# A convolution with max pooling: warm-up products of a constant, two weight turns behind the first products, loads gated one by one

## The chip, the cores and the metric

The kernel runs on one core of a Trainium2 chip. The metric is the device time of one execution in microseconds. Lower is better.

## The reference

A 3x3 convolution with padding 1 over 16 images of 64 channels and 64x64 pixels gives 128 channels; then the maximum over 2x2 blocks is taken, all in float32.

```python
batch, c_in, h, w, c_out, k = 16, 64, 64, 64, 128, 3
...
conv[b, co] += weight[co, ci, kh, kw] * x_pad[b, ci, kh:kh+h, kw:kw+w]
...
output[b, c, i, j] = np.max(conv[b, c, i*pool_size:(i+1)*pool_size,
                                      j*pool_size:(j+1)*pool_size])
```

## The kernel before

**Tiling.** Two images lie together on the 128 partitions, 64 channels each, so a matmul takes 64 partitions and there is one for each half. The eight pairs of images are split into 4 "k" pairs and 4 "w" pairs, and every pair into 4 parts of 8 output rows; that gives 16 parts of each kind, numbered 0 to 15. An accumulator (`acc_0` to `acc_3`) holds one part of one parity of conv rows, for two images, in 4 KiB of each partition[...]. The list `free` hands them out and takes them back in program order.

**Arithmetic.** Even and odd conv rows are not computed each by itself. Combinations of rows (`ks`, `ws`, `we`, `wz`, `wy`, made from x on VectorE and GpSimd) meet combinations of the weights' three kernel rows: `G0` and `G2` are plain, `D2` is g2 - g1, `D0` is g0 - g1, and `GM` and `GP` are half of g0 + g2 minus or plus g1. One product step runs six matmuls for each block of weights (three column shifts, two image halves).

**Weights.** A block is put together in `wq`, turned on TensorE in four 128x128 transposes into an accumulator (`turn`, step "T" and the block's name) and copied to `wt` (`turn_out`, step "V" and the name).

**Steps.** The order of the whole program is written out by hand in the strings HEAD, STEADY and TAIL, and each engine runs its own instructions in that order. The steps that matter here are:

- `g0`, `g1`, `g2`: ScalarE casts of weight rows to `wq`. `D2`, `D0`, `GM`, `GP`: VectorE sums and differences (lines 350, 351, 354, 357). `GS`: GpSimd, g0 + g2 (line 352).
- `XO`, `XE`: VectorE casts of the odd and even rows of `kfirst`, the first 17 rows of the first k pair, to bfloat16 in `kx` (line 337). `X1`, `X2`: ScalarE casts of `ksecond`, the next 16 rows (line 344).
- `PA`, `PB`, `PR`: products of a k part: PA into one accumulator (12 matmuls), PB (12) and PR (6) into a second. `P2`, `P0` (6 each) go into the first accumulator of a w part, `P3`, `P1` (6 each) into its second. All are on line 183.
- `EV`/`ev`: ScalarE copies an accumulator to SBUF (line 286). `MX`/`mx`: VectorE takes the maximum of the second accumulator with it (line 299). `OD`/`od`: ScalarE copies the odd columns (line 304). `CM`/`cm`: VectorE takes the maximum over the columns, gives the accumulator back and sends the output (line 318). `SE`: ScalarE seeds a w part's second accumulator with minus the first (line 295).
- `KS`, `WS`, `E` on VectorE (E on GpSimd from part 5 on), `Z`, `Y` on GpSimd: the row combinations `ks`, `ws`, `we`, `wz`, `wy` (line 248). `on_gpsimd` makes Z and Y wait for the last `on_vector` instruction ahead of them in program order.

**Loads.** SP issues `wraw` (the weights), `kfirst`, then `wload(i)` for the parts of w pairs, and `ksecond`; they share one hardware queue. `kload` is issued by GpSimd and casts to bfloat16 as it loads. `behind(a, b)` makes instruction a wait for b. In the kernel before, `wload(0)` waits for the fourth of eight warm-up products and `ksecond` follows it; `wload(1)` to `wload(3)` wait for XO; the rest of the first k pair (`kload(0, ...)`) waits for E.0.

**Warm-up.** Eight products of a zeroed tile (line 135) run ahead of the first turn, two into each accumulator.

Of the kernel before, what the change touches and what calls it, by code (L numbers as in the profile page):

```python
# [11 lines left out]
def kernel(  # L12
# [21 lines left out]
    nc = tc.nc  # L34
    FP32 = mybir.dt.float32
    BF16 = mybir.dt.bfloat16
    MAX = mybir.AluOpType.max
    ADD = mybir.AluOpType.add
    SUB = mybir.AluOpType.subtract

    B, CI, H, W = x.shape
# [4 lines left out]
    NQ = 4  # L46
# [13 lines left out]

    acc = [psum.tile([128, 2, R, W], FP32, name=f"acc_{i}") for i in range(4)]
    free = deque(range(4))
    unset = set()

# [3 lines left out]
    def behind(inst, other):  # L70
        if other is not None:
            tc.add_manual_dep(inst.ins, other.ins.name, SYNC, reason="order")

    def on_vector(inst):
        sbuf_op[0] = inst
        return inst

    def on_gpsimd(inst):
        behind(inst, sbuf_op[0])
        return inst  # L80


    def rows_of(p, lo, hi):
        return x[2 * p : 2 * p + 2].rearrange("b c h w -> (b c) h w")[:, lo:hi, :]

    def chunk(q):
        return (2 * R * q + (q > 0), min(H, 2 * R * (q + 1) + 1))
# [4 lines left out]
    def kload(j, lo, hi):  # L92
        if j not in kx:
            kx[j] = kx_pool.tile([128, H, W], BF16, name="kx")
        return nc.gpsimd.dma_start(out=kx[j][:, lo:hi, :], in_=rows_of(2 * j, lo, hi))  # L95

    def wload(i):
        j, q = divmod(i, NQ)
        lo, hi = chunk(q)
        return nc.sync.dma_start(  # L100
            out=wx[j % 2][:, lo + 1 : hi + 1, :], in_=rows_of(2 * j + 1, lo, hi)
        )
# [6 lines left out]
    klo2, khi2 = chunk(1)  # L109
    ksecond = const.tile([128, khi2 - klo2, W], FP32)  # L110
# [10 lines left out]
    D2, G0, D0, G2, GM, G1, GP = range(1, 29, 4)  # L121
    BLOCKS = {"D2": D2, "G0": G0, "D0": D0, "G2": G2, "GM": GM, "G1": G1, "GP": GP}
    wq = const.tile([CO, 29, CI], BF16)
    wt = const.tile([128, 28, CO], BF16)
    gsum = const.tile([CO, 3, CI], FP32)
# [3 lines left out]
    g0, g1, g2 = wv[:, 0:3, :], wv[:, 3:6, :], wv[:, 6:9, :]  # L129

    def slots(m):
        return wq[:, m : m + 3, :]

    def zero(t, h):
        return nc.tensor.matmul(  # L135
            acc[t][:, h], zeros[:, 0:128], zeros, start=True, stop=True, skip_group_check=True
        )

    turned = {}

    def turn(m):
        t = free.popleft()
        turned[m] = t
        unset.add(t)
        tp = acc[t][:, 0].rearrange("p a b -> p (a b)").bitcast(BF16)
        lo, hi = BLOCKS[m] - 1, BLOCKS[m] + 3
        for j in range(lo, hi):
            nc.tensor.transpose(
                tp[:, (j - lo) * 128 : (j - lo + 1) * 128],
                wq[:, j : j + 2, :].rearrange("a b c -> a (b c)"),  # L150
                ident,
            )

    def turn_out(m):
        t = turned[m]
        free.append(t)
        lo, hi = BLOCKS[m] - 1, BLOCKS[m] + 3
        src = acc[t][:, 0].rearrange("p a b -> p (a b)").bitcast(BF16)[:, 0 : (hi - lo) * 128]
        dst = wt[:, lo:hi, :].rearrange("p a b -> p (a b)")
        if m == "GM":  # L160
            nc.scalar.mul(dst, src, 0.5)
        elif m == "GP":
            nc.vector.tensor_scalar_mul(out=dst, in0=src, scalar1=0.5)  # L163
        elif m in ("G0", "G1", "G2"):
            nc.scalar.copy(out=dst, in_=src)
        else:
            nc.vector.tensor_copy(out=dst, in_=src)  # L167
# [66 lines left out]
    def row_out(name, i):  # L234
        j, q = divmod(i, NQ)
        if (name, j) not in row:
            row[name, j] = row_pool.tile([128, HO, W], BF16, name=name)
        return row[name, j][:, q * R : (q + 1) * R, :]

    def row_in(t, first, pad):  # L240
        a = first + pad
        return t[:, a : a + 2 * R - 1 : 2, :]

    def row_op(engine, name, i, a, b, op):
        j, q = divmod(i, NQ)
        t, pad = (kx[j], 0) if name == "ks" else (wx[j % 2], 1)
        f = 2 * R * q
        return engine.tensor_tensor(  # L248
            out=row_out(name, i), in0=row_in(t, f + a, pad), in1=row_in(t, f + b, pad), op=op
        )  # L250

    def ks(i):
        on_vector(row_op(nc.vector, "ks", i, 0, 1, ADD))

    def ws(i):
        on_vector(row_op(nc.vector, "ws", i, 0, 1, ADD))
# [1 line left out]
    def we(i):  # L258
        if i < 5:
            inst = on_vector(row_op(nc.vector, "we", i, 1, 0, SUB))  # L260
            if i == 0:
                behind(kload(0, chunk(2)[0], H), inst)
        else:
            on_gpsimd(row_op(nc.gpsimd, "we", i, 1, 0, SUB))

# [69 lines left out]
    def cast_rows(first):  # L335
        inst = on_vector(
            nc.vector.tensor_copy(out=kx[0][:, first:khi:2, :], in_=kfirst[:, first:khi:2, :])  # L337
        )
        if first == 1:
            for i in range(1, NQ):  # L340
                behind(wload(i), inst)

    def cast_more(first):
        nc.scalar.copy(out=kx[0][:, klo2 + first : khi2 : 2, :], in_=ksecond[:, first::2, :])
# [2 lines left out]
        "g0": lambda: nc.scalar.copy(out=slots(G0), in_=g0),  # L347
        "g1": lambda: nc.scalar.copy(out=slots(G1), in_=g1),
        "g2": lambda: nc.scalar.copy(out=slots(G2), in_=g2),
        "D2": lambda: on_vector(nc.vector.tensor_sub(out=slots(D2), in0=g2, in1=g1)),  # L350
        "D0": lambda: on_vector(nc.vector.tensor_sub(out=slots(D0), in0=g0, in1=g1)),
        "GS": lambda: on_gpsimd(nc.gpsimd.tensor_tensor(out=gsum, in0=g0, in1=g2, op=ADD)),
        "GM": lambda: on_vector(
            nc.vector.tensor_sub(out=slots(GM), in0=gsum, in1=g1)  # L354
        ),
        "GP": lambda: on_vector(
            nc.vector.tensor_add(out=slots(GP), in0=gsum, in1=g1)  # L357
        ),
        "XO": lambda: cast_rows(1),
        "XE": lambda: cast_rows(0),  # L360
        "X1": lambda: cast_more(0),
        "X2": lambda: cast_more(1),
        "PA": pa, "PB": pb, "PR": pr, "P0": p0, "P1": p1, "P2": p2, "P3": p3,
        "KS": ks, "WS": ws, "E": we, "Z": wz, "Y": wy, "SE": seed,
        "EV": lambda i, h=None: evac(("k", i), h), "ev": lambda i, h=None: evac(("w", i), h),
        "MX": lambda i, h=None: rowmax(("k", i), h), "mx": lambda i, h=None: rowmax(("w", i), h),
# [3 lines left out]
    for m in BLOCKS:  # L370
        steps["T" + m] = lambda m=m: turn(m)
        steps["V" + m] = lambda m=m: turn_out(m)

    HEAD = """
        D2 g0 D0 g2 GS g1 TD2 VD2 TG0 VG0 XO TD0 VD0 TG2 VG2 TG1 VG1 XE GM PA.0 GP TGM VGM TGP
        KS.0 E.0 WS.0 PB.0 EV.0 X1 Z.0 Y.0 VGP P2.0 MX.0 SE.0 X2 PA.1 EV.1 WS.1 KS.1 E.1 PR.0
        P0.0 P3.0 Z.1 Y.1 OD.0 CM.0 P2.1 ev.0 PB.1 SE.1 mx.0 P0.1 P1.0 MX.1 P3.1 ev.1 od.0 PR.1
        WS.2 KS.2 E.2 Z.2 Y.2 OD.1 cm.0 CM.1 PA.2 EV.2 P2.2 PB.2 SE.2 mx.1 P1.1 P0.2 MX.2 P3.2
        od.1 ev.2 cm.1 E.3 KS.3 WS.3 Z.3 Y.3 PR.2 PA.3 OD.2 CM.2 P2.3 mx.2 EV.3 PB.3 SE.3 P1.2
# [12 lines left out]
    """  # L392
    FIRST, LAST = 4, 12

    for n in range(8):
        warm = zero(n // 2, n % 2)
        if n == 3:
            behind(wload(0), warm)
            nc.sync.dma_start(out=ksecond, in_=rows_of(0, klo2, khi2))
    kx[0] = kx_pool.tile([128, H, W], BF16, name="kx")  # L400

    def run(order):
# [44 lines left out]
```

## Time and profile before

| | |
|---|---|
| median of 6 runs | 107.76 us (107.58 to 108.36) |
| the profiled execution | 107.51 us |
| its span, from first to last instruction | 105.7 us |
| TensorE busy (matmuls) | 98.6 us, 93% of the span |
| VectorE, ScalarE, GpSimd busy | 82.7, 72.6, 60.2 us |
| granted TensorE clock, mean | 0.987 |
| moved by DMA | 21.96 MB, 208 GB/s in the mean |

The span is a little shorter than the time of the execution, since 1.81 us lie around it. In lines of the profile, L183 is a line of the kernel's source, and "out<-in" names what an instruction writes and reads; many steps share a line, since a helper issues them, so steps are told apart by their tiles and their order in time. A bracket behind a line is idle time ahead of an instruction and what ended it. Busy time of a matmul is modelled; the distance between starts is the better measure of its cost.

### The profile page before, as it was taken

How to read it: one execution, taken by the hardware profiler on the slowest of the kernel's cores; microseconds unless marked ns; L12 is line 12 of the kernel's file. 1: busy time of each engine (PE TensorE's matmuls, PEld its weight loads, DVE VectorE, ACT ScalarE, POOL GpSimd, SP SyncE). 2: the span in 40 equal slices, each digit the busy share in tenths (PEclk: the TensorE clock that was granted, in tenths of full speed). 3: DMA queues.
4: the chain of work that ended last, by engine and by line, in shares of the span. 5: the costliest groups of instructions: out<-in, count | busy, mean ns of one | idle time of the engine just before them, and what ended most of it. 6: DMA issues, size and time to landing. Idle time of an engine off the chain costs nothing.

```text
span 105.7 us, 2338 instructions
## 1 busy us (share of the span) xinstructions
PE 98.6 (93%) x900; PEld 45.3 (43%) x900; DVE 82.7 (78%) x113; ACT 72.6 (69%) x92; POOL 60.2 (57%) x69
## 2 busy tenths in 40 slices
PE   5989989999999999999999999999999999999810
PEld 2544344444454444444444444444444444455400
DVE  1599989889797868697887868687969878676950
ACT  4658966776767677767767676777776676775820
POOL 6206582914429494949476594949294856745000
PEclk9999999999999999999999999999999999999995
DMA  3999989899978679999955698999968412232052
GB/s 62 339 363 329 285 214 191 164 303 291 287 269 192 210 169 157 207 362 225 304 211 163 209 194 182 243 280 208 372 233 175 152 57 102 99 105 99 0 198 99
DMA packets 12475, 21.96 MB, mean 208 GB/s; under 512 B 944, under 2 KB 9136, under 8 KB 12464
## 3 DMA queue, kind: packets, MB, share of 16 engines
q1 hardware_dynamic: 11312, 18.03, 54.2%
q0 software_dynamic: 1008, 3.65, 19.6%
q8 instruction: 7, 0.11, 0.4%
q10 hardware_dynamic: 144, 0.13, 0.4%
q14 instruction: 4, 0.03, 0.1%
HBM read 17.07 MB, written 8.39 MB: 241 GB/s over the span
## 4 chain that ended last, share of the span: by engine, by line
PE 77%; DVE 13%; DMA 4%; issue 1%; ACT 1%; SPq 0%; DVEq 0%
PE acc L183 77%; DVE acc L299 6%; DMA kfirst<-in_x_dram 4%; DVE ws L248 2%; DVE kx L337 1%; DVE we L248 1%; DVE o L318 1%; DVE ks L248 1%; ACT od L304 1%; DVE wq L357 0%; DVE wq L354 0%; SPq L105 0%; DVE wt L163 0%; DVE wt L167 0%; DVEq L299 0%
## 5 line engine op out<-in xcount | busy, mean ns | idle before, releaser
L183 PEld LDWEIGHTS <-wt 64*128 64x128 bf16 x864 | 42.6, 94 | 51.5 <-issue 1.1
L299 DVE TENSOR_TENSOR acc<-acc,ev 128x1024 f32<-128x1024 f32 (+1 forms) x34 | 39.5, 1165 | 12.2 <-PE acc L183 11.9
L183 PE MATMUL acc<-kx,wt 64*128 64x504 bf16 (+3 forms) x384 | 46.2, 373 | 0.4 <-DVE kx L337 0.4
L286 ACT COPY ev<-acc 128x1024 f32<-128x1024 f32 (+1 forms) x34 | 32.6, 964 | 12.5 <-PE acc L183 11.0
L248 POOL TENSOR_TENSOR wz<-wx 128x512 bf16<-128x512 f32 x16 | 20.4, 1272 | 30.1 <-DVE ws L248 23.3
L304 ACT COPY od<-acc 128x512 f32<-128x512 f32 x32 | 18.8, 587 | 11.6 <-PE acc L183 11.5
L318 DVE TENSOR_TENSOR o<-acc,od 128x512 f32<-128x512 f32 x32 | 21.9, 690 | 3.6 <-ACT od L304 3.6
L248 POOL TENSOR_TENSOR wy<-wx 128x512 bf16<-128x512 f32 x16 | 20.3, 1270 | 0.0
L295 ACT ACTIVATE acc<-acc 128x1024 f32<-128x1024 f32 x16 | 16.1, 1008 | 1.3 <-PE acc L183 0.9
L248 POOL TENSOR_TENSOR we<-wx 128x512 bf16<-128x512 f32 x11 | 14.1, 1278 | 0.1
L183 PE MATMUL acc<-ws,wt 64*128 64x504 bf16 (+1 forms) x96 | 13.0, 377 | 0.4 <-DVE acc L299 0.4
L183 PE MATMUL acc<-we,wt 64*128 64x504 bf16 (+1 forms) x96 | 13.0, 377 | 0.3 <-DVE we L248 0.3
L183 PE MATMUL acc<-ks,wt 64*128 64x504 bf16 (+1 forms) x96 | 13.0, 377 | 0.1
L183 PE MATMUL acc<-wy,wt 64*128 64x504 bf16 (+1 forms) x96 | 13.0, 377 | 0.0
L183 PE MATMUL acc<-wz,wt 64*128 64x504 bf16 (+1 forms) x96 | 13.0, 377 | 0.0
L248 DVE TENSOR_TENSOR ws<-wx 128x512 bf16<-128x512 f32 x16 | 12.2, 764 | 0.0
L248 DVE TENSOR_TENSOR ks<-kx 128x512 bf16<-128x512 bf16 x16 | 6.7, 416 | 0.0
L95 POOL DMA_DIRECT2D kx<-in_x_dram x7 | 4.2, 594 | 3.2 <-DVE we L248 3.2
L135 PE MATMUL acc<-zeros 128*128 128x512 bf16 x8 | 3.3, 588 | 1.2 <-DVE zeros L112 1.2
L248 DVE TENSOR_TENSOR we<-wx 128x512 bf16<-128x512 f32 x5 | 3.4, 683 | 0.0
L350 DVE TENSOR_TENSOR wq<-wraw 128x192 bf16<-128x192 f32 x1 | 0.5, 501 | 2.5 <-DMA wraw<-in_weight_dram 2.5
L135 PEld LDWEIGHTS <-zeros 128*128 128x128 bf16 x8 | 1.0, 141 | 2.8 <-issue 1.7
(26 smaller groups left out, 16.8 us busy)
## 6 DMA issues: line engine op xcount, KB each, us to landing
out_dram<-o SPq DMA_DIRECT2D x31, 256.0 KB, 3.6
wx<-in_x_dram SPq DMA_DIRECT2D x8, 512.0 KB, 6.0
wx<-in_x_dram SPq DMA_DIRECT2D x4, 544.0 KB, 5.7
kx<-in_x_dram POOLq DMA_DIRECT2D x4, 496.0 KB, 8.1
wx<-in_x_dram SPq DMA_DIRECT2D x4, 480.0 KB, 5.2
kx<-in_x_dram POOLq DMA_DIRECT2D x3, 528.0 KB, 7.6
kfirst<-in_x_dram SPq DMA_DIRECT2D x1, 544.0 KB, 4.3
ksecond<-in_x_dram SPq DMA_DIRECT2D x1, 512.0 KB, 5.6
```

Of the source, the lines that this page charges most:

```text
L95: return nc.gpsimd.dma_start(out=kx[j][:, lo:hi, :], in_=rows_of(2 * j, lo, hi))
L135: return nc.tensor.matmul(acc[t][:, h], zeros[:, 0:128], zeros, start=True, stop=True, skip_group_check=True)
L183: nc.tensor.matmul(dst[:, half, i0:i1, o0:o1], wt[lo : lo + CI, m0 + kw - half, :], rows(lo, i0, i1, c0, c1), start=start and kw == 1, sto ...
L248: return engine.tensor_tensor(out=row_out(name, i), in0=row_in(t, f + a, pad), in1=row_in(t, f + b, pad), op=op)
L286: nc.scalar.copy(out=ev[g][:, halves(h)], in_=acc[ta[g]][:, halves(h)])
L295: nc.scalar.mul(acc[t], acc[ta["w", i]], -1.0)
L299: nc.vector.tensor_tensor(out=t, in0=t, in1=ev[g][:, halves(h)], op=MAX)
L304: nc.scalar.copy(out=od[g][:, halves(h)], in_=acc[tb[g]][:, halves(h), :, 1::2])
L318: nc.vector.tensor_tensor(out=o, in0=acc[tb[g]][:, s, :, 0::2], in1=od[g][:, s], op=MAX)
L337: nc.vector.tensor_copy(out=kx[0][:, first:khi:2, :], in_=kfirst[:, first:khi:2, :])
L350: "D2": lambda: on_vector(nc.vector.tensor_sub(out=slots(D2), in0=g2, in1=g1)),
```

## The change

- The eight warm-up products read a one-element constant, broadcast, that the program's start has written, and no longer the zeroed tile. `wload(0)` still waits for the fourth.
- The turns of G1 and GP move behind PB.0, into the two halves of one accumulator; VG1 moves from ScalarE to VectorE, and stands with VGP ahead of MX.0. An accumulator is given back by VGP and no longer by VG1 and VGP each.
- `ksecond` waits for D2; `wload(1)` waits for GM; `kload(0, ...)` waits for KS.0; `wload(2)` and `wload(3)` wait for E.0.
- In HEAD, GM comes ahead of XE, E.0 and WS.0 come behind TGP, SE.0 comes ahead of MX.0, and E.1 KS.1 WS.1 take the place of WS.1 KS.1 E.1.

```diff
+    def turned_cols(m):
+        lo, hi = BLOCKS[m] - 1, BLOCKS[m] + 3
+        tp = acc[turned[m]][:, int(m == "GP")].rearrange("p a b -> p (a b)").bitcast(BF16)
+        return lo, hi, tp[:, 0 : (hi - lo) * 128]
+
     def turn(m):
-        t = free.popleft()
-        turned[m] = t
-        unset.add(t)
...
+        turned[m] = turned["G1"] if m == "GP" else free.popleft()
+        unset.add(turned[m])
+        lo, hi, tp = turned_cols(m)
...
     def turn_out(m):
-        t = turned[m]
-        free.append(t)
...
+        if m != "G1":
+            free.append(turned[m])
+        lo, hi, src = turned_cols(m)
...
-        elif m in ("G0", "G1", "G2"):
+        elif m in ("G0", "G2"):
             nc.scalar.copy(out=dst, in_=src)
         else:
             nc.vector.tensor_copy(out=dst, in_=src)
...
     def ks(i):
-        on_vector(row_op(nc.vector, "ks", i, 0, 1, ADD))
+        inst = on_vector(row_op(nc.vector, "ks", i, 0, 1, ADD))
+        if i == 0:
+            behind(kload(0, chunk(2)[0], H), inst)
...
             if i == 0:
-                behind(kload(0, chunk(2)[0], H), inst)
+                for n in range(2, NQ):
+                    behind(wload(n), inst)
...
-        if first == 1:
-            for i in range(1, NQ):
-                behind(wload(i), inst)
+
+    def load_second(inst):
+        behind(nc.sync.dma_start(out=ksecond, in_=rows_of(0, klo2, khi2)), inst)
...
-        "D2": lambda: on_vector(nc.vector.tensor_sub(out=slots(D2), in0=g2, in1=g1)),
+        "D2": lambda: load_second(
+            on_vector(nc.vector.tensor_sub(out=slots(D2), in0=g2, in1=g1))
+        ),
...
-        "GM": lambda: on_vector(
-            nc.vector.tensor_sub(out=slots(GM), in0=gsum, in1=g1)
+        "GM": lambda: behind(
+            wload(1), on_vector(nc.vector.tensor_sub(out=slots(GM), in0=gsum, in1=g1))
         ),
...
     HEAD = """
-        D2 g0 D0 g2 GS g1 TD2 VD2 TG0 VG0 XO TD0 VD0 TG2 VG2 TG1 VG1 XE GM PA.0 GP TGM VGM TGP
-        KS.0 E.0 WS.0 PB.0 EV.0 X1 Z.0 Y.0 VGP P2.0 MX.0 SE.0 X2 PA.1 EV.1 WS.1 KS.1 E.1 PR.0
+        D2 g0 D0 g2 GS g1 TD2 VD2 TG0 VG0 XO TD0 VD0 TG2 VG2 GM XE PA.0 TGM GP KS.0 PB.0 VGM
+        EV.0 TG1 TGP E.0 WS.0 X1 P2.0 VG1 Z.0 Y.0 VGP SE.0 MX.0 X2 PA.1 EV.1 E.1 KS.1 WS.1 PR.0
...
+    ones = nc.const_aps.tensor(1.0, [128, 512], BF16)
     for n in range(8):
-        warm = zero(n // 2, n % 2)
+        warm = nc.tensor.matmul(
+            acc[n // 2][:, n % 2], ones[:, 0:128], ones, start=True, stop=True, skip_group_check=True
+        )
         if n == 3:
             behind(wload(0), warm)
-            nc.sync.dma_start(out=ksecond, in_=rows_of(0, klo2, khi2))
```

The set `unset`, which starts with all four accumulators after the change, decides only whether a seed step has to clear its accumulator with products of zeros first; no seed step does so before.

More of the change, by code (lines that the diff above doesn't have):

```diff
@@ L62 @@
     free = deque(range(4))
-    unset = set()
+    unset = set(range(4))
     SYNC = mybir.DependencyInfo(mybir.DependencyClass.Sync, mybir.DependencyReason.DATA)
@@ L139 @@
     turned = {}
+    def turned_cols(m):
+        lo, hi = BLOCKS[m] - 1, BLOCKS[m] + 3
+        tp = acc[turned[m]][:, int(m == "GP")].rearrange("p a b -> p (a b)").bitcast(BF16)
+        return lo, hi, tp[:, 0 : (hi - lo) * 128]
     def turn(m):
-        t = free.popleft()
-        turned[m] = t
-        unset.add(t)
-        tp = acc[t][:, 0].rearrange("p a b -> p (a b)").bitcast(BF16)
-        lo, hi = BLOCKS[m] - 1, BLOCKS[m] + 3
+        turned[m] = turned["G1"] if m == "GP" else free.popleft()
+        unset.add(turned[m])
+        lo, hi, tp = turned_cols(m)
         for j in range(lo, hi):
@@ L154, in turn_out @@
     def turn_out(m):
-        t = turned[m]
-        free.append(t)
-        lo, hi = BLOCKS[m] - 1, BLOCKS[m] + 3
-        src = acc[t][:, 0].rearrange("p a b -> p (a b)").bitcast(BF16)[:, 0 : (hi - lo) * 128]
+        if m != "G1":
+            free.append(turned[m])
+        lo, hi, src = turned_cols(m)
         dst = wt[:, lo:hi, :].rearrange("p a b -> p (a b)")
```

## The prediction

> **What bounds the kernel now.** I read the chain of waits first, then the timelines of single engines over the first 16 us. The chain (start, duration, what):
>
> ```profile
> 1.19 4.28 DMA kfirst<-in_x_dram
> 5.47 0.02 issue
> 5.49 0.43 DVE kx L337
> ...
> 9.44 1.23 DVE acc L299
> 10.67 1.87 DVE ws L248
> 12.54 0.34 DVE ks L248
> 12.88 0.61 DVE we L248
> 13.49 0.05 issue
> 13.53 77.55 PE acc L183 x720
> ```
>
> From 13.53 us on TensorE is the chain: 720 products in 77.55 us, 0.1077 us each, without a hole. What the change can win lies before 13.53, and it passes to the end one to one as long as that stretch stays dense. Two things hold the head: the landing of kfirst (5.47), and VectorE's row of work up to E.1 (the "we" that ends at 13.49). TensorE's timeline shows what they cost:
>
> ```profile
> 4.33 1.29 PE L148 MATMUL acc<-ident,wq 128*128 128x128 bf16 x20
> 5.97 1.39 PE L183 MATMUL acc<-kx,wt 64*128 64x512 bf16 x12 [0.36 <-DVE kx L337]
> 7.30 0.62 PE L148 MATMUL acc<-ident,wq 128*128 128x128 bf16 x8
> 7.85 1.47 PE L183 MATMUL acc<-kx,wt 64*128 64x512 bf16 x12
> ...
> 13.53 0.82 PE L183 MATMUL acc<-we,wt 64*128 64x512 bf16 x6 [0.32 <-DVE we L248]
> ```
>
> PA.0 starts at 5.97 (I call this t0). Up to P2.1 at 13.53 lie 60 products (6.46) and 8 turns (0.55 from 7.30 to 7.85), 7.0 us of work; so about 0.5 us is lost ahead of P2.1. Why E.1 is late, VectorE's and GpSimd's timelines say:
>
> ```profile
> 10.58 1.96 DVE L248 TENSOR_TENSOR ws<-wx 128x512 bf16<-128x512 f32 x1
> 10.71 1.27 POOL L248 TENSOR_TENSOR wy<-wx 128x512 bf16<-128x512 f32 x1
> ```
>
> WS.1 takes 1.96 us where its kind has a median of 0.684. Its load is no reason: wx part 1 was issued at 5.95 and took 4.3 us, so landed at 10.25. It ends 0.56 us after wy (10.71 + 1.27 = 11.98).
>
> **What the Trainium skill says.** (1) "SBUF — State Buffer", Who interferes with whom: a VectorE instruction with two SBUF inputs contends with a GpSimd instruction that reads SBUF and one of them waits; one with at most one SBUF input, outside the two-port modes, doesn't. The trace agrees: 1.96 against 0.684, beside wy. (2) "DMA: Bandwidth & Descriptors", Queues, rings and completion order: each DMA engine takes descriptors of a ring in order. The trace agrees: the SP loads of the head land in issue order, at 5.47 (kfirst), 7.71 (3.11 + 4.6), 9.08 (3.48 + 5.6), 10.25, about 12.2 (6.4 + 5.8) and 13.3 (6.8 + 6.5), not all at once. (3) "TensorE: Matmul & The Clock Gate", Part 1: the array runs at half clock until a free-running window of about 3.4 us was busy. The weight loads of the warm-up are 0.43 us apart, the transposes behind it 0.064 (1.29/20); so the full clock came at about 4.1.
>
> **The change, part by part.** Times are after t0 where they have a plus.
>
> *Warm-up.* TensorE waited until 1.19 for the memset of zeros (0.86 + 0.27). A constant written at 0.31 lets it begin at about 0.8, where SP and ScalarE begin (0.74): 0.4 earlier, ending near 4.1. But TD2 starts at 4.33 with D2's wq in (3.68 + 0.50 = 4.18), so it moves to about 4.25, and the turns wait for kfirst afterwards. Worth nothing on the path; cover is kfirst. No row shows products of a constant: between a clock released earlier (nothing on the path) and twice the time (8 x 0.43 = 3.4 us late). I take the zeros' duration, the shape being the same.
>
> *Loads.* wx part 0 hangs on the fourth warm-up product and goes out at about 2.7, not 3.11. ksecond waits for D2, 4.23 for 3.48; it stands behind wx part 0 in the ring, whose data end near 6.2 (1.41 MB from the start by the GB/s of half-microsecond windows), so it lands near 9.08 as before; X1, its first reader, starts at +3.18 (9.15) and PA.1 needs X1 by +4.18, so 0.3 late costs nothing. The full 0.75 late would cost 0.35. wx part 1 waits for GM (about 6.7 for 5.95) and ksecond's data keep the ring busy until about 7.7: same landing near 10.3, E.1 wants it at 11.4. The kx load on GpSimd's queue moves from E.0 to KS.0, 8.75 to about 7.85; its 0.70 us stand ahead of Z.0, which waits for WS.0 (9.03) anyhow. wx parts 2 and 3 wait for E.0, about 8.5 and 8.9 for 6.4 and 6.8, wanted at 16.8 and later: nothing. On SP's queue nothing else waits until the output at 14.11.
> For kfirst in-order rings mean that neither ksecond's absence nor wx part 0's earlier issue moves it: t0 stays. Bounds: XO can't start before VD2 has passed (4.67 + 0.35 = 5.02), 0.47 earlier; if the 0.3 MB left of kfirst at 3.5 were shared half and half with wx part 0, it would land at about 6.0, 0.5 later.
>
> *TG1 behind PB.0.* Its four turns (4 x 0.068 = 0.27) were hidden ahead of kfirst and now lie on the path. TensorE: PA.0 to +1.33, TGM +1.60, PB.0 +2.91, TG1 and TGP +3.46, P2.0 +4.11. VG1 (0.42) goes from ScalarE, which stood idle 1.19 us before VGM, to VectorE, ahead of VGP and MX.0. From before: XO to WS.0's end is -0.48 to +3.06. VG1 follows TG1 (+3.18 plus 0.17, as VD2 behind TD2): +3.35; VGP +3.71 to +4.13; MX.0 +4.19 to +5.42 (before +3.47). G1 and GP share a tile, so PA.1, its next owner, waits for both copies: +4.18, 0.07 late. PR.0 wants MX.0: +5.48, even with PA.1's end. So VectorE's extra copy fits almost exactly.
>
> *E.1 first.* Z.0 follows WS.0 at +3.1, Y.0 ends at +5.64 (2 x 1.27). E.1 is ready at +5.42, held by wy until +5.64, ends at +6.25; KS.1 +6.6, WS.1 +7.2. TensorE goes PR.0 +6.13, P0.0 +6.78, P3.0 +7.43, P2.1 at +7.43 without a hole, to +8.08. PB.1 needs CM.0's tile: SE.0 on ScalarE +4.37, X2 +5.29, EV.1 +5.80, OD.0 +6.71 to +7.31, CM.0 +7.34 to +8.02, PB.1 at +8.09. Before, PB.1 began at 14.19, or +8.22. From there order and waits are as before (P0.1 follows PB.1 by 1.33, held by SE.1 in both).
>
> **Sum.** The hole of 0.5 goes; 0.27 of turns, 0.07 at PA.1 and the rest in CM.0 take its place: 8.22 - 8.09 = 0.13 us gained, t0 unmoved. The profiled execution took 107.51 (span 105.7 and 1.81 around it), so 107.38; the median of the six runs is 0.25 above it, 107.76, so 107.63, and I say 107.6. About 0.5%, 0.54 us, is what a measurement can tell from no change here.
>
> **Rivals.**
> A, kfirst lands earlier. For it: in 4.5 to 5.5 the DMA engines are 0.82 busy, and kfirst lands about 1 us after its bytes could be through, so stragglers were competing with later loads. Against: the in-order landings, and wx part 0 comes sooner. With VD2 as the new bound: 0.47 + 0.13 = 0.60 gained, 107.15. Chance 0.22.
> B, slower: VG1 and VGP are held by Z.0. Both engines then need the shared port; it decides if VG1, at +3.35, finds Z.0 (+3.1 to +4.4) on it. VG1 would start at +4.4, VGP end at +5.2, PA.1 wait until +5.25, 1.07 later, and everything with it: 107.63 + 1.07 = 108.7. For it: WS.1's 1.96 shows the port's price. Against: VD2 ran 0.43 beside GpSimd's gsum (4.68 to 5.51), VD0 0.42 without, and a copy out of PSUM has no SBUF input. Lesser forms (Y.0 late, E.1 held longer, CM.0 late) push the same way. Chance 0.14.
> C, slower by the clock or the constant: warm-up now ends before TD2, and the transposes have holes; if the window closes cold, up to 3.4 us run at half rate, 1.7 us lost: 109.3. Against: TensorE starts 0.4 earlier, and the clock came within 2.9 us of its start. Chance 0.09.
> The forecast itself, including t0 moved by 0.2 to 0.5 either way, has 0.55.
>
> **Numbers.** Faster 0.22 (A), same 0.55, slower 0.23 (B, C). The range, 106.9 to 108.8, takes in A with 0.25 of run-to-run spread, and B; C and half of what exceeds A are left out. The likeliest case alone: 107.3 to 108.1.
>
> **What would show it.** Right: the first warm-up product near 0.8; the XO cast near 5.5; eight turns between PB.0 and P2.0; E.1 ended before 12.4 and no idle ahead of P2.1; PB.1 about 8.1 after PA.0; the dense stretch unchanged. Wrong: the XO cast at 5.1 (A) or near 6; a VG1 or VGP of over 0.8 us or PA.1 past +4.6 (B); turns at 0.107 us or PA.0's products 0.2 apart (C); X1 waiting for ksecond past 9.5; a hole later than PB.1.

## The result: 0.4% slower, and the profile after

The changed kernel takes 108.24 us in the median, the kernel before, run beside it, 107.80. The ratio is 1.0039, with a 95% interval of 1.0023 to 1.0055: 0.42 us more, between 0.25 and 0.59. The forecast was 107.6, a gain of 0.13. The range held the time, but the sign was wrong. The ratio leaves out four of the changed kernel's 30 runs, which took 109.7 to 111.4 us where the rest took 107.7 to 109.1.

The profiled execution took 108.66 us, with a span of 106.9. The chain of waits of the changed kernel (start, duration, what):

```profile
1.18 5.17 DMA kfirst<-in_x_dram
6.34 0.02 issue
6.37 0.44 DVE kx L342
...
10.64 0.42 DVE wt L169
11.06 0.34 DVE wt L165
11.41 0.05 issue
11.45 80.80 PE acc L185 x750
```

The chain no longer goes through WS.1, KS.1 and E.1 to P2.1. It goes through two copies of turned weights (VG1 on L169, VGP on L165) to PA.1, and TensorE is dense from there, 30 products earlier in the order than before. TensorE's timeline of the changed kernel (start, duration, operation, count, idle time ahead and what ended it):

```profile
4.38 1.66 PE L151 MATMUL acc<-ident,wq 128*128 128x128 bf16 x16
6.85 1.39 PE L185 MATMUL acc<-kx,wt 64*128 64x512 bf16 x12 [0.80 <-DVE kx L342]
8.17 0.40 PE L151 MATMUL acc<-ident,wq 128*128 128x128 bf16 x4
8.50 1.47 PE L185 MATMUL acc<-kx,wt 64*128 64x512 bf16 x12
9.90 0.62 PE L151 MATMUL acc<-ident,wq 128*128 128x128 bf16 x8
10.46 0.82 PE L185 MATMUL acc<-we,wt 64*128 64x512 bf16 x6
11.45 1.47 PE L185 MATMUL acc<-kx,wt 64*128 64x512 bf16 x12 [0.17 <-DVE wt L165]
...
14.70 0.81 PE L185 MATMUL acc<-we,wt 64*128 64x512 bf16 x6
15.35 1.46 PE L185 MATMUL acc<-kx,wt 64*128 64x512 bf16 x12
```

PA.1 and PB.1 of the kernel before stand in its timeline at:

```profile
9.81 1.47 PE L183 MATMUL acc<-kx,wt 64*128 64x512 bf16 x12
...
14.19 1.46 PE L183 MATMUL acc<-kx,wt 64*128 64x512 bf16 x12
```

Two numbers are to be read here. PA.0 (12 products at 6.85) to PA.1 (12 at 11.45) is 4.60 us, where it was 9.81 - 5.97 = 3.84. PA.0 to PB.1 (12 at 15.35) is 8.50, where it was 14.19 - 5.97 = 8.22. The hole ahead of P2.1 is gone (14.70 follows 14.05 without a pause), and more than it held has come in ahead of PA.1. This pair of executions lies 1.15 us apart, more than the medians do: 0.28 is the longer way from PA.0 to PB.1, and the rest is PA.0's own start, 6.85 for 5.97, since kfirst took 5.17 us to land and not 4.28.

VectorE's timeline of the changed kernel shows what PA.1 waited for:

```profile
10.64 0.42 DVE L169 COPY wt<-acc 128x512 bf16<-128x512 bf16 x1 [0.76 <-ACT kx L349]
10.98 0.42 DVE L165 TENSOR_SCALAR wt<-acc 128x512 bf16<-128x512 bf16 x1
11.31 1.22 DVE L304 TENSOR_TENSOR acc<-acc,ev 128x1024 f32<-128x1024 f32 x1
12.44 0.68 DVE L250 TENSOR_TENSOR we<-wx 128x512 bf16<-128x512 f32 x1
```

VectorE stood idle for 0.76 us ahead of VG1. The bracket names X1 on ScalarE, but that is only what ended last. In the program VG1 waits for the semaphore count that the last turn of GP raises, though it reads only G1's half of the accumulator; the last turn of G1 raises no count of its own.

**All profiles together.** The time of the profiled execution less the start of PB.1 is 107.51 - 14.19 = 93.32 us for the kernel before and 108.66 - 15.35 = 93.31 for the changed one. Over the experiments below it lies between 93.28 and 93.38. So everything that these profiled executions gain or lose happened ahead of PB.1, and two terms describe it: when PA.0 starts, and how long PA.0 to PB.1 takes. The first differs from run to run with the landings and the clock. The second is steadier (8.50, 8.50 and 8.51 in three kernels with the turns as changed), but it too grows in an execution in which a load comes late, as g1 and g3 show below.

### The profile page after: what moved, and what is told of

Same layout as the page of the kernel before. It is cut to its first block, busy times and chain, and to the rows that moved or that the text cites. A ratio compares the mean times of both kernels' runs of the same rounds, so it can differ in the third digit from the quotient of the medians.

```text
span 106.9 us, 2334 instructions
## 1 busy us (share of the span) xinstructions
PE 99.8 (93%) x900; PEld 45.9 (43%) x900; DVE 81.9 (77%) x114; ACT 72.4 (68%) x91; POOL 60.2 (56%) x69
## 4 chain that ended last, share of the span: by engine, by line
PE 81%; DVE 7%; DMA 5%; ACT 2%; issue 1%; SPq 0%; DVEq 0%
PE acc L185 81%; DMA kfirst<-in_x_dram 5%; DVE acc L304 5%; ACT ev L291 1%; DVE o L323 1%; ACT wt L163 1%; ACT od L309 1%; ACT kx L349 0%; DVE kx L342 0%; DVE wt L169 0%; SPq L105 0%; DVE wt L165 0%; PE acc L151 0%; DVEq L304 0%
## 5 line engine op out<-in xcount | busy, mean ns | idle before, releaser
L309 ACT COPY od<-acc 128x512 f32<-128x512 f32 x32 | 18.8, 587 | 11.5 <-PE acc L185 11.5
L250 DVE TENSOR_TENSOR ws<-wx 128x512 bf16<-128x512 f32 x16 | 11.0, 685 | 0.0
L404 PE MATMUL acc<-const-bfloat16-1.0 128*128 128x512 bf16 x8 | 3.6, 628 | 0.8 <-PEq L437 0.8
L151 PEld LDWEIGHTS <-wq 128*128 128x128 bf16 x28 | 2.2, 119 | 1.7 <-issue 1.3
L151 PE MATMUL acc<-ident,wq 128*128 128x128 bf16 x28 | 2.7, 259 | 0.0
```

Of the source, the lines that this page charges most:

```text
L151: nc.tensor.transpose(tp[:, (j - lo) * 128 : (j - lo + 1) * 128], wq[:, j : j + 2, :].rearrange("a b c -> a (b c)"), ident,)
L250: return engine.tensor_tensor(out=row_out(name, i), in0=row_in(t, f + a, pad), in1=row_in(t, f + b, pad), op=op)
L309: nc.scalar.copy(out=od[g][:, halves(h)], in_=acc[tb[g]][:, halves(h), :, 1::2])
L404: warm = nc.tensor.matmul(acc[n // 2][:, n % 2], ones[:, 0:128], ones, start=True, stop=True, skip_group_check=True)
```

## The experiments

I had three theories. TURNS: the turns and copies behind PB.0 lengthen PA.0 to PB.1. LOAD, later called DELAYED KFIRST: the earlier wx part 0 delays kfirst. CLOCK: the array is still at half clock when the turns run. What the new gates of the loads do was a fourth question. Ratios are to the kernel before, run beside each, with 95% intervals.

### One part of the change alone: e1_turns, e2_loads, e3_const

**e1_turns** keeps the zeroed warm-up and the loads of before, and has the new HEAD, the shared accumulator and VG1 on VectorE.

> The new order of HEAD, the shared accumulator of G1 and GP and VG1 on VectorE, but the zeroed warm-up and the loads gated as before. Theory TURNS (the two turns behind PB.0, with VG1 waiting for the last turn of GP, lengthen the way from PA.0 to PB.1 from 8.22 to 8.50 us): 0.3 us slower than before, ratio 1.0026, and PA.1 4.6 us behind PA.0 where it was 3.84. Theory LOAD (wx part 0, issued 0.43 us earlier, delays kfirst, 6.35 for 5.47): nothing of the loss is here; the recorded forecast for this head is then 0.13 us faster, ratio 0.9988. Theory CLOCK (the constant's products leave the array at half clock for the turns): as LOAD.

Measured: 0.9994 (0.9962 to 1.0025). The loss that TURNS expected does not show in the time; its 1.0026 lies just outside the interval. The profile does show the longer way: PA.1 at 10.87 and PB.1 at 14.77 with PA.0 at 6.27, so 4.60 and 8.50, the same as in the changed kernel.

**e2_loads** is the kernel before with the new gates alone.

```diff
-            nc.sync.dma_start(out=ksecond, in_=rows_of(0, klo2, khi2))   # behind wload(0)
+        "D2": lambda: load_second(...)            # ksecond behind D2
-            for i in range(1, NQ): behind(wload(i), inst)                # behind XO
+        "GM": lambda: behind(wload(1), ...)       # wx part 1 behind GM; parts 2, 3 behind E.0
-                behind(kload(0, chunk(2)[0], H), inst)                   # behind E.0
+            behind(kload(0, chunk(2)[0], H), inst)                       # behind KS.0
```

> Only the gates of the loads: ksecond behind D2, wx part 1 behind GM, kx behind KS.0, wx parts 2 and 3 behind E.0; wx part 0 still behind the fourth product of zeros, order and turns as before. TURNS and CLOCK: no change, ratio within 0.9985 to 1.0015. LOAD in its narrow form (only the earlier wx part 0 hurts): no change or a little faster, since ksecond no longer follows kfirst closely; kfirst lands at 5.2 to 5.5. If the gates themselves starve the DMA engines, X1 waits for ksecond, and the time goes up by 0.2 to 0.4 us.

Measured: 1.0038 (1.0009 to 1.0066), slower. The chain of waits of e2_loads:

```profile
7.36 5.58 DMA wx<-in_x_dram
...
12.96 0.69 DVE ws L248
13.65 0.34 DVE ks L248
13.99 0.61 DVE we L248
...
14.64 7.56 PE acc L183 x67
```

It was wx part 1, which I hadn't named, and not ksecond: issued behind GM at 7.36 it landed at 12.94, and in the order of before WS.1, KS.1 and E.1 stand behind it. The same run shows the half clock: its 20 turns took 2.29 us (0.107 from one to the next), where the kernel before took 1.29 (0.056), and PA.0 waited for them until 6.81 although XO's cast had ended at 6.01.

**e3_const** is the kernel before with the warm-up alone: the constant for the zeroed tile, wx part 0 and ksecond still behind the fourth product.

> Only the warm-up: eight products of the constant, from 0.78 us, and with the fourth of them wx part 0 and ksecond 0.43 us earlier. LOAD: kfirst lands 0.2 to 0.9 us later, PA.0 at 6.2 to 6.9, the time 0.2 to 0.9 us up, ratio 1.002 to 1.008. CLOCK: the turns 0.10 us each and ended near 6.0, and the time up by 0.1 to 0.4 even where kfirst lands at 5.5. TURNS: no change.

Measured: 0.9994 (0.9971 to 1.0016); kfirst landed at 1.18 + 4.45 = 5.63, the 20 turns took 1.81 us, PA.0 came at 6.14 and PB.1 8.17 behind it. In the order of before the constant, with the earlier wx part 0, shows no cost: LOAD expected 1.002 or more, which lies outside the interval. So LOAD and CLOCK don't explain the loss by themselves.

### G1 turned early again, under three sets of loads

**e4_g1_early** is the changed kernel with one part undone.

```diff
-        ... TG2 VG2 GM XE PA.0 TGM GP KS.0 PB.0 VGM
-        EV.0 TG1 TGP E.0 WS.0 X1 P2.0 VG1 Z.0 Y.0 VGP SE.0 ...
+        ... TG2 VG2 TG1 VG1 GM XE PA.0 TGM GP KS.0 PB.0 VGM
+        EV.0 TGP E.0 WS.0 X1 P2.0 Z.0 Y.0 VGP SE.0 ...
-        turned[m] = turned["G1"] if m == "GP" else free.popleft()
+        turned[m] = free.popleft()
-        elif m in ("G0", "G2"):
+        elif m in ("G0", "G1", "G2"):
```

> The changed kernel, but with G1 turned ahead of PA.0 as before, copied by ScalarE, and GP alone behind PB.0 in an accumulator of its own; warm-up and loads as changed. TURNS: worked out as the recorded forecast was, PA.1 3.83 us behind PA.0 and PB.1 7.9 behind it where the changed kernel has 8.50: 0.6 us faster than the changed kernel, near 107.6, ratio to before 0.998. LOAD or CLOCK alone: little is won back against the changed kernel, ratio to before near 1.004.

Measured: 0.9996 (0.9961 to 1.0032), 0.43% below the changed kernel's 1.0039. It isn't the 0.998 that TURNS expected; the interval is wide and overlaps the changed kernel's, and the median of its 14 runs, 108.19, is no better, so its time alone proves little. The profile says more: PA.0 came at 5.89, PB.1 at 13.91, which is 8.02, 0.48 us less than 8.50. PA.1 came 4.14 behind PA.0, not 3.83, since X1 waited for ksecond until 9.36.

**f1_early_oldloads** and **f2_oldloads** are e4_g1_early and the changed kernel, both with the loads of before (all but the time of wx part 0).

```diff
-        "D2": lambda: load_second(...)
+            nc.sync.dma_start(out=ksecond, in_=rows_of(0, klo2, khi2))   # right behind wload(0)
-        "GM": lambda: behind(wload(1), ...)
-                for n in range(2, NQ): behind(wload(n), inst)            # behind E.0
+            for i in range(1, NQ): behind(wload(i), inst)                # behind XO
-            behind(kload(0, chunk(2)[0], H), inst)                       # behind KS.0
+                behind(kload(0, chunk(2)[0], H), inst)                   # behind E.0
```

> The changed order and the constant's warm-up, but G1 turned ahead of PA.0 in an accumulator of its own, and every load but wx part 0 gated as before (ksecond right behind wx part 0, wx parts 1 to 3 behind XO, kx behind E.0). Theory TWO COSTS (the turns behind PB.0 cost 0.28 us in every run; the gates leave the rings idle at 7 to 8.5 us and make later runs of waits): both are gone, PB.1 8.0 us behind PA.0 as in e4_g1_early, and the spread of e3_const: median 107.5 to 107.6, ratio 0.997 to 0.9985, lowest near 107.2. Theory DELAYED KFIRST (what is lost is the landing of kfirst by the earlier wx part 0): no better than before.

> The changed kernel with only the gates of the loads undone (as in f1_early_oldloads); turns behind PB.0 and the constant's warm-up stay. TWO COSTS: near e1_turns, median 107.95, lowest 107.7, about 0.3 us below the changed kernel's median and 0.2 above before. DELAYED KFIRST: still near 108.24, as the constant's warm-up and its early wx part 0 remain.

Measured, one after the other on one chip: f1 0.9992 (0.9968 to 1.0017), f2 1.0034 (1.0012 to 1.0056), 0.42% apart. f2 has PA.0 to PB.1 at 15.17 - 6.66 = 8.51. So undoing the loads wins nothing back, undoing the turns does. In the two profiles only 0.17 us of this lies between PA.0 and PB.1 (8.34 in f1); PA.0 itself came 0.71 us earlier in f1. And f1 fell short of its forecast of 0.997 to 0.9985. VectorE's timeline of f1:

```profile
11.01 1.69 DVE L249 TENSOR_TENSOR we<-wx 128x512 bf16<-128x512 f32 x1
...
13.56 0.68 DVE L319 TENSOR_TENSOR o<-acc,od 128x512 f32<-128x512 f32 x1
```

and GpSimd's:

```profile
8.91 0.70 POOL L95 DMA_DIRECT2D kx<-in_x_dram  x1 [3.53 <-DVE we L249]
9.63 1.28 POOL L249 TENSOR_TENSOR wz<-wx 128x512 bf16<-128x512 f32 x1
10.86 1.27 POOL L249 TENSOR_TENSOR wy<-wx 128x512 bf16<-128x512 f32 x1
```

E.1 took 1.69 us beside wy, as WS.1 took 1.96 in the kernel before: it ends 0.57 us after wy (12.70 against 12.13). The kx load, gated by E.0, holds GpSimd from 8.91 to 9.61 ahead of wz and wy; CM.0 then ends at 14.24 and PB.1 waits for it, 8.34 behind PA.0. The change had cured this by gating kx behind KS.0, and I had undone that too: wz starts 3.18 us behind PA.0 in the changed kernel, 3.68 in f1.

**g3_best** and **g4_best_fourth** gate kx as changed again: f1_early_oldloads with kx behind KS.0; g3_best also has wx part 0 behind the fifth product.

```diff
-                behind(kload(0, chunk(2)[0], H), inst)                   # behind E.0
+            behind(kload(0, chunk(2)[0], H), inst)                       # behind KS.0
-        if n == 3:
+        if n == 4:                                                       # g3_best alone
```

> f1_early_oldloads with two edits: kx behind KS.0, as in the changed kernel, so that GpSimd starts Z.0 and Y.0 0.5 us earlier and E.1 isn't held by wy; and wx part 0 behind the fifth product. PB.1 8.0 us behind PA.0 where f1_early_oldloads has 8.34 and before 8.22; with kfirst at 5.6 the median is 107.4, ratio 0.996 to 0.998. If the gates of the loads were what made the changed kernel slow, this is no better than f1_early_oldloads.

> g3_best with wx part 0 behind the fourth product, as changed. TURNS: as g3_best, ratio 0.996 to 0.998. DELAYED KFIRST: 0.2 us above g3_best.

Measured on one chip: g3_best 0.9959 (0.9935 to 0.9984), median 107.63 beside 107.85, the only kernel here whose whole interval lies below 1; g4_best_fourth 0.9999 (0.9976 to 1.0023), short of the 0.998 of TURNS; it lies above g3, as DELAYED KFIRST expected, though the two intervals overlap. g4 has PB.1 8.02 behind PA.0 (14.44 - 6.42) and started late, its 20 turns taking 2.29 us. In g3's profiled run wx part 0 landed late (3.10 + 5.31 = 8.41), E.0 waited for it, wy came late and E.1 took 1.81 us beside it; so PB.1 came 8.45 behind PA.0 and not the 8.0 expected. How often that happens no run here shows.

**h2_best_loads** is g3_best with the turns as changed (the diff of e4_g1_early, reversed).

> g3_best with the turns of G1 and GP as changed (both behind PB.0 in one accumulator, VG1 on VectorE): the loads are the same, only the turns differ. If the turns cost what PA.0 to PB.1 says (8.50 for 8.0 us): 0.45 us above g3_best, ratio to before near 1.000. If g3_best owes its gain to the loads: as fast as g3_best, 0.996.

Measured: 1.0013 (0.9996 to 1.0031), median 107.92; PA.0 to PB.1 is 14.91 - 6.23 = 8.68 with a PA.0 that itself took 0.17 longer, its second pair of products coming 0.40 us behind the first and not 0.22, and PA.1 again waits for VGP. Against g3_best's 0.9959, measured on another chip, the turns cost 0.54%. Under three sets of loads the same part costs 0.43, 0.42 and 0.54%. Each of these differences is uncertain by 0.3 to 0.4 points; that the three agree is what carries weight.

### Which gates: f3_early_gates, f4_late_gates

Both start from the changed kernel. f3 keeps the early gates, f4 the late ones:

```diff
# f3_early_gates
-        "GM": lambda: behind(wload(1), ...)
+        "GM": lambda: load_rest(...)              # wload(1), wload(2), wload(3)
-            behind(kload(0, chunk(2)[0], H), inst)                       # behind KS.0
+                behind(kload(0, chunk(2)[0], H), inst)                   # behind E.0
# f4_late_gates
-        "D2": lambda: load_second(...)
+            nc.sync.dma_start(out=ksecond, in_=rows_of(0, klo2, khi2))   # right behind wload(0)
-        "GM": lambda: behind(wload(1), ...)
+            behind(wload(1), inst)                                       # behind XO
```

> The changed kernel, with ksecond behind D2 and wx part 1 behind GM as changed, but wx parts 2 and 3 right behind part 1, and kx behind E.0 as before. If the early gates make the loss of the loads (wx part 1 out at 7.4 to 7.6, landing near 12, E.1 waits for it): stays at the changed kernel's 108.2. If the late ones do it (kx and wx parts 2, 3 out together at 9 and landing past 18, where KS.2 and PA.2 want kx): falls to 107.95.

> The opposite half: ksecond right behind wx part 0 and wx part 1 behind XO as before, but kx behind KS.0 and wx parts 2 and 3 behind E.0 as changed. Early gates to blame: 107.95. Late gates to blame: 108.2, and kx landing at 17.5 to 18.2.

Measured: f3 1.0071 (1.0031 to 1.0111), f4 1.0037 (1.0018 to 1.0056). Neither half wins back what I expected: f4 stays at the changed kernel's 1.0039, and f3 is worse: behind GM and followed at once by parts 2 and 3, wx part 1 takes 6.90 us to land (13.59), and E.1 waits 1.8 us for it. The profile of f4 is of an execution of 110.22 us and is not read for the loads; in it TensorE stood idle for 1.58 us between the last turn and PA.0, and PA.0's 12 products then took 2.52 us for 1.39, at a granted clock of 0.50 from 7 to 10 us. That is what rival C feared, in one execution.

### wx part 0 later: g1_wx0_fifth

The changed kernel with `if n == 4:` for `if n == 3:` ahead of `behind(wload(0), warm)`.

> The changed kernel with one digit changed: wx part 0 waits for the fifth warm-up product, not the fourth, so that it goes out at 3.1 us as before the change and not at 2.7. Theory TURNS (all of the loss is the 0.28 us between PA.0 and PB.1, plus a gain of 0.1 to 0.2 that the forecast counted on): no change, ratio to before near 1.004, PB.1 8.50 us behind PA.0. Theory DELAYED KFIRST (wx part 0's earlier issue costs 0.2 us of kfirst's landing in the middle run): ratio near 1.002 and kfirst landing below 5.8.

Measured: 1.0030 (1.0007 to 1.0052), told apart neither from 1.0039 nor from the 1.002 of DELAYED KFIRST. kfirst landed at 5.2 and PA.0 came at 5.70, but PA.1 then waited for X1 (ksecond landed at 9.8) and E.1 0.85 us for wx part 1, and PB.1 came 8.82 behind PA.0. With an early PA.0 the gated loads are what is late next. VectorE's timeline of g1 also settles the wrong name in the bracket above:

```profile
9.50 0.42 DVE L169 COPY wt<-acc 128x512 bf16<-128x512 bf16 x1 [0.76 <-PE acc L151]
```

and ScalarE's:

```profile
9.81 0.62 ACT L349 CAST kx<-ksecond 128x512 bf16<-128x512 f32 x1 [0.84 <-DMA ksecond<-in_x_dram]
```

VG1 starts before X1 does: it waits for the turns, not for X1.

### The copies on the path: g2_vg1_scalar, h1_p2_between

**g2_vg1_scalar** gives VG1 back to ScalarE (`elif m in ("G0", "G1", "G2")`), nothing else.

> The changed kernel with VG1 copied by ScalarE (idle between X1 and SE.0) and not by VectorE. Both copies can start when the last turn of GP is through. If VectorE's chain VG1, VGP, MX.0 behind that turn is what holds PA.1: PA.1 4.4 us behind PA.0 for 4.60, PB.1 8.33 for 8.50, ratio to before near 1.0023. If the turns' own time on TensorE were all of it: PA.1 stays at 4.60.

Measured: 1.0049 (1.0023 to 1.0075), slower, against my forecast. VectorE's timeline of g2:

```profile
10.59 0.42 DVE L165 TENSOR_SCALAR wt<-acc 128x512 bf16<-128x512 bf16 x1 [1.58 <-ACT wt L167]
```

The copies don't run side by side. VGP waits for VG1's end on ScalarE (9.97 + 0.58 = 10.55), then starts. That both write `wt` is not the reason: in the kernel before VD0 runs on VectorE (5.83 to 6.25) beside ScalarE's three copies to `wt` (5.00 to 6.55), each out of an accumulator of its own. What VG1 and VGP have in common besides is the accumulator they read, and in the program of g2 VGP's one wait is for VG1. PA.1 goes from 4.60 to 4.90 behind PA.0, PB.1 from 8.50 to 8.79. So the chain is last turn of GP, VG1, VGP, PA.1, one after the other, and a longer VG1 goes on to PB.1 one to one.

**h1_p2_between** moves P2.0 between TG1 and TGP (`EV.0 TG1 E.0 WS.0 X1 P2.0 TGP VG1`).

> The changed kernel with P2.0 between the turns of G1 and those of GP; the work of each engine stays the same. If VG1 waits for the last turn of GP, though it reads only G1's half of the accumulator: VG1 starts 4.4 us behind PA.0 (3.79 in the changed kernel), PA.1 at 5.2 (4.60), PB.1 at 9.1 (8.50), and the time is up by 0.6 us on the changed kernel, ratio to before 1.009 to 1.01. If VG1 waits for G1's own turns only: VG1 at 3.5, PA.1 at 4.9, ratio near 1.006.

Measured: 1.0109 (1.0086 to 1.0131). TensorE's timeline of h1:

```profile
6.58 1.39 PE L185 MATMUL acc<-kx,wt 64*128 64x512 bf16 x12 [0.52 <-DVE kx L342]
...
9.63 0.40 PE L151 MATMUL acc<-ident,wq 128*128 128x128 bf16 x4
9.96 0.82 PE L185 MATMUL acc<-we,wt 64*128 64x512 bf16 x6
10.72 0.40 PE L151 MATMUL acc<-ident,wq 128*128 128x128 bf16 x4
12.04 1.47 PE L185 MATMUL acc<-kx,wt 64*128 64x512 bf16 x12 [0.93 <-DVE wt L165]
```

G1's turns are through by 10.03 (9.63 + 0.40), but VG1 starts at 11.23, 0.11 us after GP's last turn (10.72 + 0.40 = 11.12; in the changed kernel 0.12 after 9.90 + 0.62); PA.1 comes 5.46 behind PA.0, PB.1 9.36. VG1's wait for GP's turns is shown.

## Why the prediction was wrong

**Where it failed: the sum of "TG1 behind PB.0".** It had PA.1 4.18 us behind PA.0; measured 4.60, and from there PB.1 follows as worked out (1.31 for PA.1 and 24 products of 0.108, to 8.50 for 8.09). The 0.42 splits into two mis-sized terms:

- VG1 "follows TG1" was the larger one. I let it start 0.17 us after the turn of G1, reading one half of the accumulator; it starts after the last turn of GP, which stands 0.27 us later. g1, h1 and the program's own wait show it. In this program, sharing an accumulator joins the waits of both its halves.
- "0.27 of turns" was too small. Four turns between products take 0.33 (8.17 to 8.50), 0.05 more for TGM alone, and TensorE pauses 0.09 ahead of TG1 (12 products of 0.109 from 8.50 end at 9.81; TG1 starts at 9.90). P2.0 starts at 3.61, not 3.46: 0.15.

VG1 then starts at 3.79, where 3.35 was forecast (0.27 and 0.15, and 0.02 of rounding), VGP at 4.13 for 3.71, PA.1 at 4.60 for 4.18: the sentence that "VectorE's extra copy fits almost exactly" was the margin that broke. The hole that went was worth 0.48 us; the way to PA.1 grew by 0.76 (4.60 for 3.84), and 0.28 is left as a loss. What e4, f1 and g3 do with G1 early again agrees that this part is the main loss: 0.42 to 0.54%, against 0.39% for the whole change. That it is all of it isn't shown (see the start of PA.0 below).

**What held.** The hole ahead of P2.1 went, by E.1 first. The reading of WS.1's 1.96 us was right, and f1 and g3 repeated it on E.1 (1.69 and 1.81 us). The stretch behind PB.1 didn't move. VG1 and VGP took 0.42 us beside wz (10.03 to 11.29), so rival B's mechanism, the port, did not act on them, though PA.1 reached its mark of 4.6 in another way.

**The loads.** "Worth nothing" was right in the sum (f2 at 1.0034 and the changed kernel at 1.0039 can't be told apart) and wrong in a step. wx part 1 was to land near 10.3, 3.6 us after its issue; it landed at 12.06 (7.56 + 4.5; 0.88 of the delay is the late PA.0), and at about 11.2 (6.61 + 4.6) in e4. The DMA engines weren't kept busy by ksecond. The windows from 6.5 to 8.5 and 8.5 to 11.5 us of the changed kernel (the last columns are clock, DMA share and GB/s):

```profile
6.50:8.50 2.00, 1.65 (x16) 0.79 (x16) 2.00 (x6) 0.17 (x1) 0.00 (x0) 1.00 0.66 235
8.50:11.50 3.00, 2.83 (x30) 1.22 (x30) 2.24 (x6) 2.13 (x4) 2.17 (x3) 1.00 0.69 193
```

and of the kernel before:

```profile
6.50:8.50 2.00, 2.00 (x24) 0.97 (x22) 2.00 (x6) 0.81 (x3) 0.00 (x0) 1.00 0.96 347
8.50:11.50 3.00, 3.00 (x30) 1.41 (x28) 2.94 (x4) 2.68 (x4) 2.73 (x3) 1.00 1.02 356
```

The cover was the late PA.1: E.1 reached its turn at 12.44, after the landing. In the order of before (e2) that cover is missing, in f3 and g1 the landing is later than it reaches, and the wait shows.

**PA.0's start.** In the profiled run kfirst landed at 6.35 and the turns took 0.10 us each, at half clock, as rivals A (reversed) and C had it; but kfirst decided, since the turns ended near 6.05. The forecast held PA.0's start unmoved, because it took the loads on one ring to be served in the order of issue. Whether the change moves it stays open. In the 16 profiles kfirst took 4.0 to 5.2 us to land. The four landings of 4.9 us and more are all among the ten with wx part 0 out at 2.7 us; the six with it at 3.1 have 4.0 to 4.6. All turns ran at full pace in two of the three profiles with zeros, and in three of the thirteen with the constant. That is too little to decide, and one profile is one run. The times lean the same way: e1_turns, with zeros, stands at 0.9994, and f2_oldloads, which differs from it only by the constant and, with it, the earlier wx part 0 and ksecond, at 1.0034 (on another chip), though both have 8.5 us from PA.0 to PB.1; g3_best and g4_best_fourth, apart by the gate of wx part 0 alone, differ by 0.4% too. Against it stand e3_const and g1_wx0_fifth. So the turns cost what the 0.28 us says, which lies within the measured 0.25 to 0.59 by itself; a part of the loss may be the warm-up's.

## What to carry to other kernels

When two results share a buffer, work out the readers' start from the last write into any part of it, and see in the program's waits whether a reader of one half is let go early. Work moved out of an idle gap onto the busy engine costs its own time and also its copies, its consumers and the owner of the buffer it holds: the four turns of G1 cost 0.3 us on TensorE, and PA.1 came 0.76 us later with all that hangs on them. Where two engines fit with no margin, count what a small error would cost. And with another gate a load need not keep its old time to landing: wx part 1 took 4.3 us before, and 4.5, 5.6 and 6.9 in the changed kernel, e2 and f3; where the first reader had no slack the wait showed.

## What I had not expected of the hardware

Which clock the first turns run at is a matter of the run: after the same eight products of 0.43 us, 20 turns took 1.28 (f1), 1.81 (e3), 1.92 (g3) or 2.29 us (g4 with the constant, e2 with zeros). From the second turn on they follow each other at 0.107 or 0.056 us; where a run has both (e3, g3), the pace changes once, from the slow to the fast. The view of granted clock shows 1.00 while the turns run at either pace (e2 from 4.5 to 6.6 us, the kernel before from 4 to 6); only the distance between instructions tells. In g4, with 20 turns at 0.107 us, PA.0 started at 6.42, a microsecond after kfirst's landing; with 16, as changed, they end near 6.05. Turning G1 later does shorten this in such a run, and the change is slower all the same. The Trainium skill ("TensorE: Matmul & The Clock Gate", Part 1) calls the window that releases the clock free-running, so that its phase differs from run to run. The spread of the turns agrees, but it is wider than the half microsecond either way that the page gives: in f1 the pace was full by 4.21, 3.4 us after the first product, and in g4 not yet at 6.18, 5.4 us after it.
